# Start, bank choice, weight splits, filler transposes and a tail order changed together in a one-core decoder kernel

## The chip, the cores and the metric

The kernel runs on one core of a Trainium2 chip. The metric is the device time of one execution in microseconds (us); before the change its median over three runs is 1117.82 us (1117.63 to 1119.79).

The engines are named as in the profile: PE (TensorE matmul) with PEld (its weight loads), DVE (VectorE), ACT (ScalarE), POOL (GpSimd) and SP (SyncE, which here only issues DMAs).

## The reference

Two decoder layers on 256 tokens of width 1024. Each layer is FFN, mixer, FFN, per-layer input embedding, and each of the four is followed by a layer norm. The mixer of layer 0 is forgetting attention (16 heads of 64), that of layer 1 multi-head latent attention (16 heads of 128 + 64). All is float32.

```python
for i in range(DEPTH):                       # DEPTH = 2
    if i == N_A:                             # N_A = 1
        k_nope, k_rope, v_shared = shared_kv(x, ...)
    x = post_norm(x, 0.5 * swiglu(x, ffn1_w_in[i], ffn1_w_out[i]), ...)
    mix = fox_mixer(x, ...) if i < N_A else mla_mixer(x, ...)
    x = post_norm(x, mix, ...)
    x = post_norm(x, 0.5 * swiglu(x, ffn2_w_in[i], ffn2_w_out[i]), ...)
    gate = sigmoid(x @ ple_w_gate[i] + ple_b_gate[i])
    x = post_norm(x, gate * (p[i] @ ple_w_proj[i]), ...)

# fox_mixer: q, k, v = parts of x @ w_in; cum = cumsum(log_sigmoid(f_logit + b_f))
#   w = softmax(causal(q.k / 8 + cum_q - cum_k));  out = (w @ v) @ w_o
# post_norm(x, d) = layer_norm(ALPHA * x + d);  swiglu = (silu(gate) * up) @ w_out
```

## The kernel before

**Three matmuls for one.** Every float32 operand is split into a high part (rounded to the fp32r format) and a low part (the rest); a product is high x high + high x low + low x high (`mm3`). For weights the split is `Stream.split` (L140 on ACT writes the high part, L141 on DVE the low part, which reads the high part); for activations it is `parts` (L429 on ACT, L430 on DVE). A unit of weights is 128x1024 elements; two units make a group, which is what one DMA (or a few) loads into one of three raw buffers.

**The planner.** The order of instructions on every engine is the order in which the Python code emits them. `Stream` decides while emitting where the splits go: `use(key)` makes sure that a unit is split (and splits on the spot what isn't), `pump()` is called after every `mm3` and splits the next unit if a free slot is there and its own rough clocks (`pe_t`, `act_t`, `dve_t`, `arrives`) say that its data has arrived and that ACT and DVE are not behind. There are ten slots `hl0` to `hl9` for split units, and the buffers `ota`, `otb`, `qk`, `fs` are lent to it where they are not needed. DMAs go out on SP in the order of `load`.

**The start.** `setup` issues the loads: x of token tile 0 (two halves), group 0 of the first FFN's input weights in four pieces, x of tile 1. `run` transposes x of tile 0 (`XT(0)`), then `ffn(..., cold=True)` runs `H(0, 0)` (weight chunk 0, tile 0; four units of 6 matmuls of 512 columns), with `XT(1)` after its third unit, then `H(0, 1)` on the same units, then chunk 1. `spin` runs matmuls on a zero tile.

**FFN.** Chunks 0 and 1 go through `H`, chunks 2 to 10 through `HT` in three groups, 96 matmuls of 256 columns each; between the groups stand the output products `W` (matmuls of 512 columns). At the start of the second and third group (`c == group[0] > 2`), `EDGE` gives a number of transposes of the identity that are thrown away.

**Forgetting attention** (`fox`). `V(n, t)` makes the values (n: half of the heads, t: token tile) in PSUM ring "h" (two banks). `gates` makes the forget gates; their pointwise chain (`s1` to `s6`, on ACT, DVE and POOL) is put into a background list of which one piece is emitted at each `use` and at two places of each `ws`. `gen_k(j)`, `gen_q(j)` make keys and queries of a pair of heads: 24 matmuls of 256 columns (`ws`), in ring "h" too, and a split of the result (`parts`). Then a loop over eight head pairs j emits, in this order: `gen_k(j+1)`; `T(j-1)`, the transposes of the probabilities of the pair before (L897, L424) and their `parts` into PT; `QK(j)`; `softmax(j)`; `gen_q(j+1)`; `AV(j-1)`. `softmax` is: masked maxima on DVE (L865), bias (L872, L873), four exponentials on ACT (L877), one reciprocal of the four sums on DVE (L882), four multiplications on POOL (L886). In the last round and behind it the output products `O(k, t)` take the place of `gen`.

**Latent attention** (`mla`). A loop over 16 heads of the same kind (L1164, L1168, L1173, L1175 are its softmax); behind it comes a tail:

```python
self.load_gb(li, 1)
O(LATE + 2, (1,))
O(14, (0,))
T(15)
AV(15)
O(LATE + 3, (1,))
O(15, (0,))
```

The functions that the change touches:

Of the kernel before, what the change touches and what calls it, by code (L numbers as in the profile page):

```python
# [10 lines left out]
F32 = mybir.dt.float32  # L11
# [18 lines left out]
STAG = 3  # L30
LATE = 6
HAT = 12
VAT = 12
SW_COLD = 0
SW_H00 = 0
SW_H10 = 1
SW_H01 = 2
# [9 lines left out]
    (((0, 0),), ((1, 0),), ((0, 1),)),  # L47
)
GROUPS = ((2, 3, 4), (5, 6, 7), (8, 9, 10))
EDGE = {(0, "ffn1"): 4, (0, "ffn2"): 1, (1, "ffn1"): 2, (1, "ffn2"): 1}  # L50
VT = {0: (2, (0,)), 5: (2, (1,)), 8: (3, (0,)), 10: (3, (1,))}


# [13 lines left out]
class Recorder:  # L67
# [7 lines left out]
    def pump(self, *a, **k):  # L75
        pass

    lend = reclaim = check = load = busy = pair = pump


class Stream:


    def __init__(self, nc, raw_pool, pool, loads, seq):
        self.nc, self.raw_pool, self.pool, self.loads = nc, raw_pool, pool, loads
        seen = []
        self.groups = []
        for key in seq:
            g = group_of(key)
            if g not in seen:  # L90
# [20 lines left out]
        self.arrives = {}  # L111

    def load(self, n=NRAW):
        while self.loaded < len(self.groups) and self.loaded < self.done + n:
            g = self.groups[self.loaded]
            r = self.raw_pool.tile([128, 2048], F32, name="raw")
            self.loads(self.nc.sync, g, r, self.loaded < 2)
# [5 lines left out]
    def split(self):  # L123
# [16 lines left out]
        nc.scalar.activation(hi, src, AF.Copy)  # L140
        nc.vector.tensor_tensor(lo, src, hi.bitcast(F32), op=ALU.subtract)  # L141
        self.pair(n)
        self.hl[key] = w
# [43 lines left out]

    def pump(self):

        if self.ready == len(self.order) or not self.slots:  # L190
            return
        arrival = self.arrives.get(group_of(self.order[self.ready]), 1e12)
        if arrival <= self.pe_t + 500 and max(self.act_t, self.dve_t) <= self.pe_t + SLACK_NS:
            self.split()
# [29 lines left out]
def unit_of(key, raw):  # L224
# [5 lines left out]
        return raw[:, 1024 * u : 1024 * u + 1024], 128, 1024  # L230
    if k in ("fk", "fq"):
        return raw.rearrange("p (k c) -> p k c", c=256)[:, :, 128 * u : 128 * u + 128], 128, 1024
    if k == "ff":
        return raw[:, 0:1024], 128, 1024
    if k == "pb":
        return raw[0:1, 0:1024], 1, 1024
    if k == "kd":
        return raw[:, 640 * u : 640 * u + 640], 128, 640
    if k == "dq":
# [10 lines left out]
def make_loads(a):  # L250
    def rows(ap, k0, n):
        return ap[k0 * 128 : (k0 + n) * 128, :].rearrange("(k p) c -> p k c", p=128)

    def loads(q, g, raw, fine):
        k, i = g[0], g[-1]
        if k == "win":
            w = a[g[2]][0][g[1]]
            c = g[3]
            r = raw.rearrange("p (k c) -> p k c", c=512)
            n = 2 if fine else 4  # L260
            for k0 in range(0, 4, n):
                for s in range(2):
# [73 lines left out]
class Trunk:  # L336
# [33 lines left out]
    def setup(self):  # L370
# [6 lines left out]
        self.ones = one([1, 128], F32R, "ones")  # L377
        self.xT = one([128, 2, 2, 8, 128], F32R, "xT")
        self.rope = one([128, 2, 2, 64], F32, "rope")
        self.load_x(0)  # L380
        self.S.load(1)
        self.load_x(1)
        nc.gpsimd.memset(self.mask, 0.0)
        self.spin(2)
        warm = self.tl([128, 1], F32, "ss", 2)
        nc.gpsimd.memset(self.mhalf, -0.5)
# [17 lines left out]
    def load_x(self, t):  # L404
        for h in range(2):
            self.dma(
                self.x[t][:, 512 * h : 512 * h + 512],
                None if self.rec else self.a["x"][0, 128 * t : 128 * t + 128, 512 * h : 512 * h + 512],
            )


    def mm3(self, out, lhsT, rhs, start, stop):
# [17 lines left out]
        self.nc.vector.tensor_tensor(lo, src, hi.bitcast(F32), op=ALU.subtract)  # L430
        self.S.pair(cols(src))

    def transposed(self, t, src):

        for h in range(2):
# [10 lines left out]
    def XT(self, t):  # L446
        self.transposed(t, self.x[t])

    def moving(self, ps, t, name, width, at=None, what=None, sweeps=0):

# [58 lines left out]
    def ffn(self, li, which, lni, kv=False, at=None, cold=False):  # L509
# [7 lines left out]
        def H(c, t, at=None, what=None, sweeps=0):  # L517
            ps = self.bank("h")
            self.moving(ps, t, ("win", li, which, c), 512, at, what, sweeps)
            if c not in g:  # L520
                g[c] = self.tl([128, 768], F32, "P", 2)
            gt = g[c][:, 256 * t : 256 * t + 256]
# [57 lines left out]
        if kv:  # L580
            self.kv_down(0)
        if cold:
            H(0, 0, 18, lambda: self.XT(1), SW_COLD)
            H(0, 1, sweeps=SW_H01)
            H(1, 0)
        else:
            H(0, 0, sweeps=SW_H00)
# [131 lines left out]
    def fox(self, li):  # L719
# [11 lines left out]
        def ws(key, out):  # L731
            w = self.use(key)
            for k in range(8):
                if k in (3, 6) and self.bg:
                    self.bg.popleft()()
                self.mm3(
                    out, lambda i: w[:, i, 128 * k : 128 * k + 128],
                    lambda i: self.xT[:, :, i, k, :], k == 0, k == 7,
                )

        fs = self.own([128, 2048], F32, "fs")
        bf = self.tl([128, 1], F32, "bf", 1)
# [81 lines left out]
        def gen(j, key, c0):  # L824
            ps = self.bank("h")
            ws((key, j), ps[:, 0:256])
            o = qk[:, j % 2]
            self.parts(o[:, 0, c0 : c0 + 256], o[:, 1, c0 : c0 + 256], ps[:, 0:256])

        def gen_k(j):  # L830
            gen(j, "fk", 256)

        def gen_q(j):
            gen(j, "fq", 0)

        def QK(j, ring):
            sb = [self.bank(ring) for _ in range(2)]
# [17 lines left out]
        def softmax(j):  # L855
# [26 lines left out]
            nc.vector.reciprocal(su, su)  # L882
            for s in range(2):
                for q, (c0, c1) in enumerate(seg):
                    i = 2 * s + q
                    nc.gpsimd.tensor_scalar(  # L886
                        P[s][:, c0:c1], P[s][:, c0:c1], su[:, i : i + 1], 1.0, op0=ALU.mult, op1=ALU.mult
                    )
            st[j] = P

        def T(j):
# [52 lines left out]
        for j in range(8):  # L944
            if j == 2:
                self.load_gb(li, 1)
            if j < 7:
                gen_k(j + 1)
            else:
# [5 lines left out]
                S.lend("fs")  # L955
            if j >= 1:
                T(j - 1)
            QK(j, "y" if j < 7 else "h")
            softmax(j)
            if j < 7:  # L960
                gen_q(j + 1)
            else:
                O(2, 0)
                O(3, 0)
            if j >= 1:
                AV(j - 1)
        S.lend("qk")
        O(4, 0)
        O(5, 0)
# [80 lines left out]
    def mla(self, li):  # L1050
# [221 lines left out]

    def run(self):
        S = self.S
        self.XT(0)
        self.spin(2)
# [74 lines left out]
```

## Time and profile before

| | us |
|---|---|
| median of three runs | 1117.82 |
| the profiled execution, its own time | 1116.59 |
| its span, first to last instruction | 1114.8 |
| PE busy | 1087.3 |
| PEld busy | 982.3 |
| DVE busy | 712.2 |
| ACT busy | 541.6 |
| POOL busy | 81.8 |

The profiled execution took 1.8 us more than its span and 1.2 us less than the median. PE's matmuls overlap in the records, so PE busy time counts a stretch of back-to-back matmuls as full, at whatever rate they run; the number of matmuls in a stretch shows the rate. In a row of the timeline stand the start, the length, the engine, the line, the operation, output <- inputs, the shape and the count, and in brackets the idle time before it with what ended that.

Where the stages lie (us from the start of the span): first FFN 0 to 190, forgetting attention 190 to 320, second FFN 320 to 510, embedding 510 to 545, first FFN of layer 1 545 to 730, latent attention 730 to 890, second FFN 890 to 1075, embedding to the end.

### The profile page before, as it was taken

The page shows a single profiled execution, that of the slowest core. Times are in us where ns is not written, and L with a number is a line of the kernel's source. Part 1 is how long each engine was busy: PE and PEld are TensorE (multiplying, and loading weights), DVE is VectorE, ACT ScalarE, POOL GpSimd, SP SyncE. Part 2 cuts the span into 40 slices and gives each one's busy share as a digit, 9 for nine tenths or more (in the row PEclk, how much of TensorE's full clock was granted, in tenths as well). Part 3 has the DMA queues.
Part 4 walks back from the last instruction along what each step waited for, and adds up shares of the span by engine and source line. Part 5 has one row for each costly group of instructions (what it writes and reads, how often), then busy time and mean ns, then how long its engine had stood idle before and what let it go on. Part 6 is the DMA issues. An engine that isn't in the chain of part 4 may idle for free. (4 is left out here: it accounts for less than half of the span.)

```text
span 1114.8 us, 17666 instructions
## 1 busy us (share of the span) xinstructions
PE 1087.3 (98%) x7182; PEld 982.3 (88%) x7182; DVE 712.2 (64%) x994; ACT 541.6 (49%) x786; POOL 81.8 (7%) x130
## 2 busy tenths in 40 slices
PE   8999999989999999999999999998999899999997
PEld 6999998889879989897899899987899689898986
DVE  5765545777787555457976454397766786454576
ACT  5554433566646435443565343345655455344421
POOL 0000000322200000000320000011111000000000
PEclk9999999989999999999999999999999999999999
DMA  9796652554338666454486655344443478555402
GB/s 299 240 308 212 216 188 68 171 168 152 114 113 301 200 209 199 159 175 157 155 287 229 204 186 166 88 111 145 156 123 114 158 257 278 185 190 189 164 26 76
DMA packets 150548, 199.00 MB, mean 179 GB/s; under 512 B 11714, under 2 KB 128450, under 8 KB 150468
## 3 DMA queue, kind: packets, MB, share of 16 engines
q1 hardware_dynamic: 150468, 197.88, 53.8%
q8 instruction: 56, 0.92, 0.3%
q14 instruction: 24, 0.20, 0.1%
HBM read 196.81 MB, written 1.05 MB: 177 GB/s over the span
## 5 line engine op out<-in xcount | busy, mean ns | idle before, releaser
L141 DVE TENSOR_TENSOR hl<-raw,hl 128x1024 fp32r<-128x1024 f32 (+3 forms) x295 | 349.3, 1202 | 184.8 <-ACT hl L140 183.7
L140 ACT ACTIVATE hl<-raw 128x1024 fp32r<-128x1024 f32 (+3 forms) x295 | 298.5, 1032 | 208.0 <-PE y L420 85.3
L420 PE MATMUL h<-xT,hl 128*128 128x256 f32 x2016 | 243.3, 281 | 2.4 <-DVE g L430 1.8
L420 PEld LDWEIGHTS h<-xT,hl 128*128 128x128 f32 x2016 | 237.4, 190 | 4.7 <-DVE g L430 2.0
L420 PE MATMUL y<-hl,g 128*128 128x512 f32 x816 | 189.6, 390 | 0.0
L420 PEld LDWEIGHTS y<-hl,g 128*128 128x128 f32 x816 | 152.2, 188 | 31.0
L420 PE MATMUL h<-hl,xT 128*128 128x512 f32 (+1 forms) x432 | 102.1, 387 | 3.3 <-DVE hl L141 1.9
L420 PE MATMUL tr<-xT,hl 128*128 128x256 f32 x864 | 102.5, 278 | 0.0
L420 PEld LDWEIGHTS tr<-xT,hl 128*128 128x128 f32 x864 | 100.5, 188 | 0.1
L420 PEld LDWEIGHTS h<-hl,xT 128*128 128x128 f32 x432 | 79.3, 188 | 21.2 <-DVE hl L141 3.0
L492 POOL TENSOR_TENSOR rs<-ve,mhalf 128x1 f32<-128x1 f32 x16 | 15.2, 950 | 829.4 <-DVE ve L491 829.4
L420 PE MATMUL y<-hl,xT 128*128 128x512 f32 (+2 forms) x276 | 52.6, 346 | 0.0
L420 PEld LDWEIGHTS y<-hl,xT 128*128 128x128 f32 x276 | 44.0, 188 | 6.4 <-issue 0.7
L429 ACT ACTIVATE xT<-tr 128x512 fp32r<-128x512 f32 x36 | 20.0, 596 | 57.0 <-PE tr L424 57.0
L430 DVE TENSOR_TENSOR g<-P,g 128x512 fp32r<-128x512 f32 x36 | 24.9, 693 | 34.5 <-ACT g L429 34.5
L429 ACT ACTIVATE g<-P 128x512 fp32r<-128x512 f32 x36 | 22.8, 632 | 40.1 <-DVE P L559 29.1
L420 PE MATMUL y<-hl,ota 128*128 128x512 f32 x144 | 36.1, 394 | 0.0
L141 DVE TENSOR_TENSOR otb<-raw,otb 128x1024 fp32r<-128x1024 f32 (+1 forms) x20 | 24.1, 1203 | 18.8 <-ACT otb L140 18.8
L141 DVE TENSOR_TENSOR qk<-raw,qk 128x1024 fp32r<-128x1024 f32 x21 | 25.9, 1233 | 14.3 <-ACT qk L140 14.3
L420 PE MATMUL tr<-xT,qk 128*128 128x256 f32 x264 | 31.9, 277 | 0.0
L420 PEld LDWEIGHTS tr<-xT,qk 128*128 128x128 f32 x264 | 30.9, 188 | 0.0
L430 DVE TENSOR_TENSOR xT<-tr,xT 128x512 fp32r<-128x512 f32 x36 | 23.1, 683 | 11.7 <-ACT xT L429 11.7
(222 smaller groups left out, 1349.2 us busy)
## 6 DMA issues: line engine op xcount, KB each, us to landing
raw<-in_ffn_w_in_dram SPq DMA_DIRECT2D x172, 512.0 KB, 4.9
raw<-in_ffn_w_out_dram SPq DMA_DIRECT2D x44, 1024.0 KB, 5.1
raw<-in_fox_w_in_dram SPq DMA_DIRECT2D x12, 1024.0 KB, 5.2
raw<-in_ple_w_gate_dram SPq DMA_DIRECT2D x8, 1024.0 KB, 5.0
raw<-in_mla_w_o_dram SPq DMA_DIRECT2D x8, 1024.0 KB, 5.5
gb<-in_ln_g_dram SPq DMA_DIRECT2D x8, 512.0 KB, 5.1
gb<-in_ln_b_dram SPq DMA_DIRECT2D x8, 512.0 KB, 7.7
raw<-in_fox_w_o_dram SPq DMA_DIRECT2D x4, 1024.0 KB, 4.8
```

Of the source, the lines that this page charges most:

```text
L140: nc.scalar.activation(hi, src, AF.Copy)
L141: nc.vector.tensor_tensor(lo, src, hi.bitcast(F32), op=ALU.subtract)
L420: self.nc.tensor.matmul(out, lhsT, rhs, start=start, stop=stop)
L429: self.nc.scalar.activation(hi, src, AF.Copy)
L430: self.nc.vector.tensor_tensor(lo, src, hi.bitcast(F32), op=ALU.subtract)
L492: nc.gpsimd.tensor_tensor(rs, ve, self.mhalf, op=ALU.pow)
```

## The change

Seven edits in one:

1. **Loads at the start.** The first two groups are loaded in pieces of one 128-row block (128 KB) instead of two; both groups are issued at once, with the four halves of x between their pieces (x tile 0 half 0 first, then blocks 0 and 1, x tile 1 half 0, blocks 2 and 3, x tile 0 half 1, block 4, x tile 1 half 1, blocks 5 to 7).
2. **`first()`** takes the place of `H(0, 0)` and `H(0, 1)`: it goes through the eight blocks with both token tiles by turns, transposes x by halves, and splits the first four units in two pieces each (`FINE`), with planned splits held.
3. **`V` for t = 1** uses a bank of ring "y" (four banks) instead of "h".
4. **Splits in the forgetting attention set by hand.** `QUIET` and `hold` keep `pump` from splitting in `gates`, `gen_k(0)`, `gen_q(0)`, the later part of `gen_k(1)`, `gen_q(1)`, and in the whole loop from j = 1. Instead, in each round one unit is split whole just ahead of the first matmuls of `gen_k` (`split_now`, from `gen_k(2)` on), and another in two halves: the high part on ACT behind `T(j-1)` (`ahead`), the low part on DVE behind the reciprocals and multiplications of `softmax(j)` (`later`). In the last round one split stands between `O(2, 0)` and `O(3, 0)`.
5. **The reciprocal** is done in two pieces, one for each head of the pair, each followed by that head's multiplications.
6. **`EDGE` of layer 1's first FFN** is 4 instead of 2.
7. **The tail of the latent attention** runs `T(15)`, `O(LATE + 3, (1,))`, `AV(15)`, `O(14, (0,))`, `O(15, (0,))`.

```diff
+FINE = 4
+QUIET = {("ff", 0): 0, ("fk", 0): 0, ("fq", 0): 0, ("fk", 1): 3, ("fq", 1): 0}
-EDGE = {(0, "ffn1"): 4, (0, "ffn2"): 1, (1, "ffn1"): 2, (1, "ffn2"): 1}
+EDGE = {(0, "ffn1"): 4, (0, "ffn2"): 1, (1, "ffn1"): 4, (1, "ffn2"): 1}
...
+    def ahead(self):
+        if self.ready == len(self.order) or not self.slots or self.rest is not None:
+            return
+        if self.arrives.get(group_of(self.order[self.ready]), 1e12) <= self.pe_t + 500:
+            self.split(half=True)
+    def split_now(self):
+        self.ahead()
+        self.later()
+    def later(self):
+        if self.rest is not None:
+            f, self.rest = self.rest, None
+            f()
...
+        if self.ready < FINE:
+            part(slice(0, 1))
+            between()
+            part(slice(1, 2))
+        elif half:
+            nc.scalar.activation(hi, src, AF.Copy)
...
+            self.rest = rest      # the low part on DVE, emitted by later()
+            return
+        else:
+            part(slice(None))
...
     def pump(self):
-        if self.ready == len(self.order) or not self.slots:
+        if self.ready == len(self.order) or not self.slots or self.hold:
...
-        self.load_x(0)
-        self.S.load(1)
-        self.load_x(1)
+        self.load_x(0, 0)
+        self.S.between = {(0, 2): lambda: self.load_x(1, 0),
+            (1, 0): lambda: self.load_x(0, 1), (1, 1): lambda: self.load_x(1, 1)}
+        self.S.load(2)
...
+        def first():
+            S.hold = True
+            self.XT(0, (0,))
+            self.spin(2)
+            S.split()
+            part(0, 0, 1)
+            S.split(lambda: self.XT(1, (0,)))
+            part(0, 2)
+            part(1, 0, 1)
+            S.split(lambda: self.XT(0, (1,)))
+            part(1, 2)
+            part(0, 3)
+            part(1, 3)
+            self.XT(1, (1,))
+            S.split()
+            part(0, 4, 5, 6, 7)
+            act(0, 0, ps[0])
+            part(1, 4, 5)
+            S.split()
+            S.split()
+            S.hold = False
+            part(1, 6, 7)
+            act(0, 1, ps[1])
...
-            ps = self.bank("h")                       # V
+            ps = self.bank("h" if t == 0 else "y")
...
+                S.hold = hold or k >= QUIET.get(key[:1] + key[-1:], 8)      # ws
...
-            nc.vector.reciprocal(su, su)
+            def divide(s):
+                nc.vector.reciprocal(su[:, 2 * s : 2 * s + 2], su[:, 2 * s : 2 * s + 2])
...
+            divide(0)
+            divide(1)
+            S.later()
...
+            S.hold = j >= 1                            # the loop over head pairs
...
                 T(j - 1)
+                if j < 7:
+                    S.ahead()
...
                 O(2, 0)
+                S.split_now()
                 O(3, 0)
...
         O(LATE + 2, (1,))                              # tail of mla
+        T(15)
+        O(LATE + 3, (1,))
+        AV(15)
         O(14, (0,))
-        T(15)
-        AV(15)
-        O(LATE + 3, (1,))
         O(15, (0,))
```

More of the change, by code (lines that the diff above doesn't have):

```diff
@@ L76, in pump @@
         pass
-    lend = reclaim = check = load = busy = pair = pump
+    lend = reclaim = check = load = busy = pair = split = ahead = later = split_now = pump
+    between, hold = {}, False
 class Stream:
@@ L111, in __init__ @@
         self.arrives = {}
+        self.between = {}
+        self.hold = False
+        self.rest = None
     def load(self, n=NRAW):
@@ L116, in load @@
             r = self.raw_pool.tile([128, 2048], F32, name="raw")
-            self.loads(self.nc.sync, g, r, self.loaded < 2)
+            self.loads(self.nc.sync, g, r, self.loaded < 2, self.between)
             self.raw[g] = r
@@ L121, in load, with split @@
             self.loaded += 1
-    def split(self):
+    def ahead(self):
[10 more added lines that the diff above has]
+            f()
+    def split(self, between=lambda: None, half=False):
+        self.later()
         nc = self.nc
@@ L252, in rows, with loads @@
         return ap[k0 * 128 : (k0 + n) * 128, :].rearrange("(k p) c -> p k c", p=128)
-    def loads(q, g, raw, fine):
+    def loads(q, g, raw, fine, between):
         k, i = g[0], g[-1]
@@ L259, in loads @@
             r = raw.rearrange("p (k c) -> p k c", c=512)
-            n = 2 if fine else 4
+            n = 1 if fine else 4
             for k0 in range(0, 4, n):
+                if fine and (i, k0) in between:
+                    between[i, k0]()
                 for s in range(2):
@@ L431, in parts, with transposed @@
         self.S.pair(cols(src))
-    def transposed(self, t, src):
-        for h in range(2):
+    def transposed(self, t, src, halves=(0, 1)):
+        for h in halves:
             tr = self.bank("tr")
@@ L519, in H, with part, act @@
             self.moving(ps, t, ("win", li, which, c), 512, at, what, sweeps)
+            act(c, t, ps)
+        def first():
+            ps = [self.bank("h") for _ in range(2)]
+            def part(t, *ks):
+                for k in ks:
+                    w = self.use(("win", li, which, 0, k // 2))
+                    for i, j in SWEEPS[0][0]:
+                        self.mm(
+                            ps[t], self.xT[:, t, i, k, :], w[:, j, 512 * (k % 2) : 512 * (k % 2) + 512],
+                            k == 0 and (i, j) == (0, 0), k == 7 and (i, j) == SWEEPS[0][0][-1],
+                        )
+                    self.S.pump()
+            S.hold = True
[20 more added lines that the diff above has]
+            act(0, 1, ps[1])
+        def act(c, t, ps):
             if c not in g:
@@ L582, in ffn @@
         if cold:
-            H(0, 0, 18, lambda: self.XT(1), SW_COLD)
-            H(0, 1, sweeps=SW_H01)
+            first()
             H(1, 0)
@@ L729, in V, with ws @@
             v[t, n] = o
-        def ws(key, out):
+        def ws(key, out, at={}, hold=False):
             w = self.use(key)
             for k in range(8):
+                if k in at:
+                    at[k]()
+                S.hold = hold or k >= QUIET.get(key[:1] + key[-1:], 8)
                 if k in (3, 6) and self.bg:
@@ L739, in ws @@
                 )
+            S.hold = hold
         fs = self.own([128, 2048], F32, "fs")
@@ L966, in fox @@
                 AV(j - 1)
+        S.hold = False
         S.lend("qk")
```

48 lines of the change are left out of this document (28 added, 20 removed).

## The prediction

> **What bounds the kernel now.** I read the page first, then the table of busy time by stretches of 20 us, then the timeline of PE wherever a stretch was not full or its matmuls were few for its length, and last the rows of DVE, ACT and POOL around each hole.
>
> ```profile
> span 1114.8 us, 17666 instructions
> PE 1087.3 (98%) x7182; PEld 982.3 (88%) x7182; DVE 712.2 (64%) x994; ACT 541.6 (49%) x786; POOL 81.8 (7%) x130
> ...
> 0.00:20.00 20.00, 15.54 (x60) 10.51 (x61) 9.68 (x11) 11.06 (x15) 1.75 (x11) 1.00 0.94 307
> 220.00:240.00 20.00, 17.68 (x140) 16.83 (x138) 14.84 (x30) 11.28 (x23) 3.78 (x6) 0.91 0.65 211
> ```
>
> PE is 98% busy, and nothing in the change removes a product: only holes, slow stretches and fillers on PE can be won. In each row the first number behind the length is PE's busy time. Of 20.00 us PE worked 15.54 at the start and 17.68 at 220, where forgetting attention begins. The number behind the five engines is the granted clock: 0.91 at 220.
>
> **1. The start.**
>
> ```profile
> 0.72 0.87 SPq L358 DMA_DIRECT2D x<-in_x_dram  x2
> x<-in_x_dram SPq DMA_DIRECT2D x1, 256.0 KB, 2.6
> 4.77 1.09 ACT L429 ACTIVATE xT<-tr 128x512 fp32r<-128x512 f32 x2 [2.56 <-PE tr L424]
> 6.52 1.06 ACT L140 ACTIVATE hl<-raw 128x1024 fp32r<-128x1024 f32 x1 [0.67 <-DMA raw<-in_ffn_w_in_dram]
> 7.63 0.50 PE L420 MATMUL h<-hl,xT 128*128 128x512 f32 x1 [1.17 <-ACT hl L140]
> 15.10 1.03 PE L424 MATMUL tr<-ident,x 128*128 128x128 f32 x8
> 15.89 18.10 PE L420 MATMUL h<-hl,xT 128*128 128x512 f32 x78
> ```
>
> Each unit's split waits for its DMA, and PE for the split. From 15.89 on PE runs through at 18.10/78 = 0.232 us a matmul; 30 of these (6 of `H(0, 0)`, 24 of `H(0, 1)`) end the first two products at 22.9.
>
> After: the first half of x lands where it does now, 0.72 + 2.6 = 3.3; its ACT eviction starts at 4.77 and is half as long, to 5.3. Block 0 needs 512 KB landed; 256 KB were there at 3.3 and 1 MB at 6.5, so about 4.4 by interpolation. Half a unit on ACT is about 0.55: first matmul at 5.9 instead of 7.63. From there lie 48 matmuls (11.1) and 12 transposes (1.03/8 each, 1.5) on PE, 18.5 in all. Followed through step by step, PE still waits some 0.9 us, mostly at block 6, whose split stands behind the fourth x eviction on ACT. So 19.4 to 19.5 against 22.9: **gain 3.3**. The twenty smaller DMAs cost about 0.45 of SP's time each (0.87/2), 9.7 us for all, and with 2.6 of landing the last arrives near 13, where it does now. If these small pieces land 2 us late, 1.2 stays; PE never waiting would give 4.3.
>
> **2. `V` in ring "y", and `QUIET`.**
>
> ```profile
> 220.15 2.91 PE L420 MATMUL h<-xT,hl 128*128 128x256 f32 x24
> 224.84 7.35 PE L420 MATMUL h<-xT,hl 128*128 128x256 f32 x48 [1.78 <-DVE g L430]
> 233.40 5.73 PE L420 MATMUL h<-xT,hl 128*128 128x256 f32 x48
> 224.11 0.68 DVE L430 TENSOR_TENSOR g<-h,g 128x512 fp32r<-128x512 f32 x1
> 227.16 0.42 DVE L430 TENSOR_TENSOR qk<-h,qk 128x256 fp32r<-128x256 f32 x1
> 224.00:230.00 6.00, 5.16 (x31) 5.16 (x32) 5.84 (x10) 3.80 (x6) 0.00 (x0) 0.72 0.63 192
> ```
>
> `gen_q(0)` wants the bank of `V(1, 1)`, whose low part DVE does only at 224.11, behind gate arithmetic and two splits: PE stands 1.78. Then the granted clock over 6 us is 0.72, and the next 48 matmuls take 7.35 where the same 48 later take 5.73: 1.62 more. With `V` in "y" that wait has no cause. Next late is `gen_k(1)`, due at about 220.15 + 2 x 2.73 = 225.6, which wants the bank of `gen_k(0)`: its low part, 0.42, comes behind the row at 224.11, two gate rows and a copy, near 226.3 without the split that stands between the gate rows now. So 0.7 stays: **gain 1.8 + 1.6 - 0.7 = 2.7** (1.1 if the clock drops all the same, 3.4 if nothing is late). Behind `gen_k(1)` are only the queue of PE and, on DVE, work for `QK(0)`, due later.
>
> **3. The first round of the softmax.**
>
> ```profile
> 238.25 3.65 POOL L886 TENSOR_SCALAR P<-P,su 128x128 f32<-128x128 f32 x4 [15.14 <-DVE su L882]
> 304.44 1.62 POOL L886 TENSOR_SCALAR P<-P,su 128x128 f32<-128x128 f32 x4 [6.47 <-DVE su L882]
> 238.97 0.50 PE L897 MATMUL tr<-ident,P 128*128 128x128 f32 x2
> 241.50 0.78 PE L897 MATMUL tr<-ident,P 128*128 128x128 f32 x2 [2.03 <-POOL P L886]
> 243.62 4.47 PE L420 MATMUL h<-xT,hl 128*128 128x256 f32 x24
> 262.08 3.01 PE L420 MATMUL h<-xT,hl 128*128 128x256 f32 x24
> 242.00:248.00 6.00, 6.00 (x42) 5.61 (x43) 4.58 (x17) 3.09 (x11) 0.08 (x1) 0.72 0.50 175
> 238.85 1.30 DVE L141 TENSOR_TENSOR hl<-raw,hl 128x1024 fp32r<-128x1024 f32 x1 [0.77 <-ACT hl L140]
> ```
>
> PE's `T(0)` waits 2.03 and some 0.3 more for POOL's third and fourth multiplications, and again a stretch at the lower clock follows (4.47 for 24 matmuls against 3.01: 1.46). The four take 3.65 where 1.62 is enough (the row at 304.44). With the reciprocal in two, the first head's two multiplications start 0.8 earlier, all four are through at about 239.1, about when the low part that begins at 238.85 could hold them, against 241.9. `T(0)` is due at 238.97; some 0.3 may stay where DVE is later with the maxima. **Gain 2.3 + 1.5 - 0.3 = 3.5** (low 1.0: a wait of 1.3 and the clock stay; high 3.8).
>
> **4. The rounds from j = 4 on.**
>
> ```profile
> L886 POOL TENSOR_SCALAR P<-P,su 128x128 f32<-128x128 f32 x1 | 1.3, 1336 | 0.0
> 266.94 0.18 DVE L882 RECIPROCAL su<-su 128x4 f32<-128x4 f32 x1 [1.11 <-ACT P L877]
> 267.82 1.29 DVE L141 TENSOR_TENSOR hl<-raw,hl 128x1024 fp32r<-128x1024 f32 x1 [0.70 <-ACT hl L140]
> 264.76 0.37 ACT L877 ACTIVATE P<-y,tt 128x128 f32<-128x128 f32 x1 [2.93 <-DVE tt L873]
> 260.26 0.60 PE L897 MATMUL tr<-ident,P 128*128 128x128 f32 x4
> 268.81 0.38 PE L897 MATMUL tr<-ident,P 128*128 128x128 f32 x2
> 278.12 0.38 PE L897 MATMUL tr<-ident,P 128*128 128x128 f32 x2
> 296.79 0.38 PE L897 MATMUL tr<-ident,P 128*128 128x128 f32 x2
> ```
>
> From one `T` to the next a round takes 8.55 where PE doesn't wait (260.26 to 268.81) and 9.31 where it does (268.81 to 278.12; to 296.79 two more of 9.33). DVE sets that: it works through but for 1.11 waiting for the exponentials and 0.70 waiting for the high part of the split. The high part goes to where ACT is idle (2.93 before the first exponential), so the 0.70 goes and a round on DVE is 9.33 - 0.70 = 8.65 with the second reciprocal (0.18) mostly in the 1.11. The four rounds that wait lose 0.8 each now, 0.1 to 0.2 then: **gain 2.6** (0.8 to 3.2).
>
> What speaks against it: while DVE's low part runs, POOL's third multiplication takes 1.336 instead of about 0.37, and now the low part comes straight behind the reciprocal, ahead of it. I take that the whole 1.2 is lost to POOL there; the second head is then ready at about 269.1 against 269.8 now, just behind `T`, which is the 0.1 to 0.2. The Trainium skill, "SBUF — State Buffer", section "Who interferes with whom", says the same: a DVE instruction with two SBUF inputs and a GpSimd one that reads SBUF exclude each other for a whole instruction, by order of issue. The trace agrees (1.336 beside a low part); without that rule nothing would stay and the sum would be 0.6 better.
>
> **5. `EDGE` 2 to 4.**
>
> ```profile
> 94.75 0.60 PE L424 MATMUL tr<-ident 128*128 128x128 f32 x4
> 106.09 11.04 PE L420 MATMUL h<-xT,hl 128*128 128x256 f32 x96
> 632.49 0.38 PE L424 MATMUL tr<-ident 128*128 128x128 f32 x2
> 705.83 11.47 PE L420 MATMUL h<-xT,hl 128*128 128x256 f32 x96
> ```
>
> The same 96 matmuls take 11.04 behind four fillers (layer 0) and 11.47 behind two (layer 1). Six chunks of layer 1 run at the slower rate: 6 x 0.43 = 2.6, less four more fillers of 0.11 (0.60 - 0.38 for two): **gain 2.15** if the rate is set by the fillers, -0.44 if not. I take the gain, since both groups of layer 0 with the same four run fast. Other groups may change their rate as well, 1.3 a group either way; I take none.
>
> **6. The tail.**
>
> ```profile
> 871.08 1.59 PE L420 MATMUL y<-hl,ota 128*128 128x512 f32 x6
> 872.66 0.82 POOL L1175 TENSOR_SCALAR P<-P,su 128x128 f32<-128x128 f32 x2 [6.69 <-DVE su L1173]
> 879.79 1.53 PE L420 MATMUL y<-hl,fs 128*128 128x512 f32 x6
> ```
>
> `O(14)` waits for the evictions of `AV(14)`, and `AV(15)` for those of `T(15)` with nothing between. After: `T(15)` waits for POOL to 873.5, `O(LATE + 3)` covers its evictions to 875.2, their low part is there at 875.5 to 876.6 (a planned split ahead of it or not), so the last product starts at 877.7 to 878.8 instead of 879.79. **Gain 1.3** (1.0 to 2.1; -0.5 if two planned splits stand ahead of PT on ACT and DVE).
>
> **The sum.** 3.3 + 2.7 + 3.5 + 2.6 + 2.15 + 1.3 = 15.6. The profiled execution took 1116.59, so 1101.0; the median of the runs is 1.2 above it: **1102 us**. The lows together give 1.2 + 1.1 + 1.0 + 0.8 - 0.4 - 0.5 = 3.2, the highs 4.3 + 3.4 + 3.8 + 3.2 + 2.15 + 2.1 = 19.
>
> **The rivals.** *The clock.* The stretches at the lower clock may not come from the waits. They would stay: 1.6 + 1.5 less, 1105. For: after four waits of 0.8 in the rounds there is none, so a wait alone doesn't do it. Against: both stand right behind the two longest waits. The Trainium skill, "TensorE: Matmul & The Clock Gate", Part 1, says that about 3.4 us of idle are needed; here 1.78 and 2.03 went ahead of a drop, so the trace doesn't bear that out.
>
> *POOL and DVE keep the rounds bound.* If low parts hold POOL's multiplications as long as at 238.25 (3.65 for 1.62), parts 3 and 4 give their lows: 1106.3. Against: only one split stands behind the reciprocals.
>
> *The waits only move*: to DMA landing at the start, from `T` to `QK`, or `EDGE` changes no rate; the lows: 1114 to 1115.
>
> *Slower: the loop runs out of split weights.* With planned splits off, `use` must split on the spot what isn't ready, PE standing for 1.06 + 1.23 = 2.3. Two units are needed and two split in a round, so this decides only if `ahead` finds no slot or no data in most rounds; then from j = 4 eight units cost 18.4, and part 4 is lost: 1102 + 18.4 + 2.6 = 1123. Against: the ten slots hold the units up to at least `fq(3)` before the loop holds the planner off, and a unit's group is loaded two groups, so about two rounds, before it is split.
>
> **How the numbers follow.** Forecast 0.62 (1098.5 to 1106), clock 0.12, POOL and DVE 0.12, waits moved 0.07, slower 0.04, better than 1098 0.03. The likeliest is 1102; 1097 to 1110 leaves out most of the moved waits, the slower and the best, 0.15 in all. A measurement here tells 0.2%, 2.2 us: faster 0.90, same 0.05, slower 0.05.
>
> **What would show it.** First matmul of weights near 6 us and chunk 1 from 19.5; no wait on `g` at 222; clock 1.00 there; `T` to `T` of 8.6 to 8.7 in all rounds; chunks of 11.04 in layer 1; 8 us or less from `O(LATE + 2)` to the last product of the tail's half. It is wrong if DVE rows of L141 inside the rounds stand ahead of the maxima, or if PE waits for L141 in `gen_k`.

## The result and the profile after

| | before | after |
|---|---|---|
| median of four runs, us (lowest to highest) | 1118.59 (1117.63 to 1119.79) | 1100.39 (1099.47 to 1102.1) |
| ratio after/before, 95% interval | | 0.984 [0.982, 0.985] |
| the profiled execution, its own time / span | 1116.59 / 1114.8 | 1102.1 / 1100.3 |
| PE / DVE / ACT / POOL busy | 1087.3 / 712.2 / 541.6 / 81.8 | 1080.1 / 711.5 / 542.5 / 79.7 |

The change made the kernel 18.2 us faster, 1.6%; predicted were 1102 and a range of 1097 to 1110. The two profiled executions differ by 14.5 us of span. The forecast of 1101.0 for the profiled execution met 1102.1.

The page after the change, and the same two stretches of busy time (behind the length: PE, PEld, DVE, ACT and POOL busy with their counts, the granted clock, the share of DMA, GB/s):

```profile
span 1100.3 us, 17702 instructions
PE 1080.1 (98%) x7186; PEld 976.7 (89%) x7186; DVE 711.5 (65%) x1006; ACT 542.5 (49%) x790; POOL 79.7 (7%) x130
...
0.00:20.00 20.00, 18.43 (x70) 12.45 (x71) 8.88 (x14) 10.39 (x17) 1.76 (x11) 1.00 0.87 275
220.00:240.00 20.00, 19.38 (x173) 18.47 (x172) 14.97 (x44) 11.92 (x30) 3.39 (x7) 1.00 0.46 148
```

PE works 18.43 of the first 20 us (15.54 before) and 19.38 of the twenty from 220 (17.68 before), there at full clock (0.91 before).

The timeline of forgetting attention after, PE first, then one round on DVE and POOL:

```profile
224.31 3.01 PE L469 MATMUL h<-xT,hl 128*128 128x256 f32 x24 [0.62 <-DVE qk L479]
234.10 0.60 PE L994 MATMUL tr<-ident,P 128*128 128x128 f32 x4
242.65 0.60 PE L994 MATMUL tr<-ident,P 128*128 128x128 f32 x4
...
257.03 0.17 DVE L976 RECIPROCAL su<-su 128x2 f32<-128x2 f32 x1 [0.93 <-ACT P L969]
257.11 1.20 DVE L175 TENSOR_TENSOR hl<-raw,hl 128x1024 fp32r<-128x1024 f32 x1
265.48 0.17 DVE L976 RECIPROCAL su<-su 128x2 f32<-128x2 f32 x1 [0.93 <-ACT P L969]
265.57 1.21 DVE L175 TENSOR_TENSOR hl<-raw,hl 128x1024 fp32r<-128x1024 f32 x1
264.65 0.83 POOL L979 TENSOR_SCALAR P<-P,su 128x128 f32<-128x128 f32 x2 [5.63 <-DVE su L976]
265.74 1.73 POOL L979 TENSOR_SCALAR P<-P,su 128x128 f32<-128x128 f32 x2 [0.26 <-DVE su L976]
```

No `T` waits. The one wait on DVE in a round is 0.93 for the exponentials, and its round is 265.48 - 257.03 = 8.45, just under PE's 8.54. POOL's second pair takes 1.73 beside the low part where the first takes 0.83, and is done at 267.47; `T` wants it at 268.26. The times from one `T` to the next, worked out from the unrounded starts of the `T` rows (L897 before, L994 after, L995 in r10):

| round from `T(j)` to `T(j+1)` | 0 | 1 | 2 | 3 | 4 | 5 | 6 | sum |
|---|---|---|---|---|---|---|---|---|
| before | 12.75 | 8.54 | 8.55 | 9.31 | 9.39 | 9.28 | 9.47 | 67.29 |
| after | 8.55 | 8.54 | 8.54 | 8.54 | 8.54 | 8.43 | 8.50 | 59.64 |
| r1, planner | 8.55 | 11.34 | 9.73 | 9.33 | 9.32 | 9.96 | 9.31 | 67.54 |
| r2, one reciprocal | 11.81 | 8.54 | 8.54 | 8.56 | 8.73 | 9.01 | 8.64 | 63.82 |
| r3, low part at once | 8.54 | 8.54 | 8.69 | 9.16 | 9.15 | 10.21 | 8.51 | 62.80 |
| r10, both parts late | 8.54 | 8.54 | 8.54 | 8.79 | 9.30 | 10.01 | 9.30 | 63.02 |

### The profile page after: what moved, and what is told of

The parts are those of the page before. It is cut to its first block, busy times and chain, and to the rows that moved or that the text cites. A ratio compares the mean times of both kernels' runs of the same rounds, so it can differ in the third digit from the quotient of the medians.

```text
span 1100.3 us, 17702 instructions
## 1 busy us (share of the span) xinstructions
PE 1080.1 (98%) x7186; PEld 976.7 (89%) x7186; DVE 711.5 (65%) x1006; ACT 542.5 (49%) x790; POOL 79.7 (7%) x130
## 3 DMA queue, kind: packets, MB, share of 16 engines
HBM read 196.81 MB, written 1.05 MB: 180 GB/s over the span
## 5 line engine op out<-in xcount | busy, mean ns | idle before, releaser
L164 DVE TENSOR_TENSOR hl<-raw,hl 128x1024 fp32r<-128x1024 f32 (+3 forms) x287 | 334.5, 1184 | 172.5 <-ACT hl L163 171.7
L163 ACT ACTIVATE hl<-raw 128x1024 fp32r<-128x1024 f32 (+3 forms) x287 | 286.9, 1021 | 198.6 <-PE y L469 82.2
L469 PE MATMUL h<-xT,hl 128*128 128x256 f32 x2016 | 239.9, 278 | 1.7 <-DVE P L613 0.7
L469 PEld LDWEIGHTS h<-xT,hl 128*128 128x128 f32 x2016 | 234.1, 188 | 3.7 <-DVE P L613 0.9
L469 PE MATMUL h<-hl,xT 128*128 128x512 f32 (+1 forms) x396 | 94.7, 388 | 0.4 <-DVE hl L164 0.3
L469 PEld LDWEIGHTS h<-hl,xT 128*128 128x128 f32 x396 | 72.1, 188 | 17.1 <-DVE hl L164 2.2
L469 PE MATMUL y<-hl,xT 128*128 128x512 f32 (+2 forms) x312 | 61.0, 351 | 0.0
L469 PEld LDWEIGHTS y<-hl,xT 128*128 128x128 f32 x312 | 50.8, 188 | 7.9 <-issue 0.7
```

What stands on the lines that cost most here:

```text
L163: nc.scalar.activation(hi[:, c], src[:, c], AF.Copy)
L164: nc.vector.tensor_tensor(lo[:, c], src[:, c], hi[:, c].bitcast(F32), op=ALU.subtract)
L469: self.nc.tensor.matmul(out, lhsT, rhs, start=start, stop=stop)
```

## The experiments

Each undoes or shifts one part of the changed kernel. A median moves by up to 2 us for reasons that lie elsewhere (end of this part), so each is read first from its own stage in the trace, against the changed kernel.

| run | what | in its stage, us | median, us | ratio to before, 95% |
|---|---|---|---|---|
| r1 | planner in the loop | +7.9 | 1106.87 | 0.992 [0.989, 0.994] |
| r2 | one reciprocal | +4.2 | 1103.56 | 0.988 [0.986, 0.991] |
| r3 | low part at once | +3.2 | 1101.85 | 0.987 [0.985, 0.989] |
| r4 | `V` in "h" | +2.8 | 1100.80 | 0.986 [0.984, 0.988] |
| r5 | old start | +1.7 | 1101.14 | 0.987 [0.985, 0.988] |
| r6 | two fillers | +2.2 | 1102.17 | 0.987 [0.986, 0.989] |
| r7 | old tail | +3.7 | 1102.83 | 0.988 [0.987, 0.990] |
| r8 | four fillers, third groups | -2.5 | 1100.00 | 0.986 [0.984, 0.987] |
| r9 | wait filled | +4.2 | 1102.63 | 0.987 [0.985, 0.989] |
| r10 | both parts late | +3.4 | 1102.86 | 0.988 [0.986, 0.990] |
| r11 | three additions | see there | 1100.88 | 0.986 [0.983, 0.988] |
| r12 | changed kernel again | | 1098.74 | 0.984 [0.982, 0.986] |

**r1, the planner back in the loop.**

```diff
-            gen(j, "fk", 256, {0: S.split_now} if j >= 2 else {}, j >= 2)
+            gen(j, "fk", 256)                     # and gen_q alike
...
-            S.hold = j >= 1
...
-                if j < 7: S.ahead()
...
-                S.split_now()
```

> The loop of the forgetting attention gives its splits back to the planner (no hold, no split set by hand); the reciprocal in two, QUIET, V in ring y and all else stay as changed. Theory A (a round is bound by DVE, and the 0.70 us that DVE stood for the high part of a split was what made it so): from the third or fourth round on T to T is 9.1 to 9.3 us again instead of 8.54, with T waiting for POOL or DVE; the kernel is 2.0 to 3.5 us slower than the changed one. Rival B (the reciprocal in two frees POOL early enough by itself, the place of the splits is nothing): T to T 8.54 to 8.6 in all rounds, no wait at T, within 0.5 us.

DVE in the second round, from `T(1)` to `T(2)`:

```profile
242.47 0.17 DVE L976 RECIPROCAL su<-su 128x2 f32<-128x2 f32 x1 [0.96 <-ACT P L969]
243.42 1.23 DVE L164 TENSOR_TENSOR fs<-raw,fs 128x1024 fp32r<-128x1024 f32 x1 [0.78 <-ACT fs L163]
244.56 1.22 DVE L164 TENSOR_TENSOR hl<-raw,hl 128x1024 fp32r<-128x1024 f32 x1
246.91 2.36 DVE L164 TENSOR_TENSOR hl<-raw,hl 128x1024 fp32r<-128x1024 f32 x2
```

Theory A's mark is there: 0.78 of DVE waiting for the high part and rounds of 9.3. But the loss is 7.9, not 2.0 to 3.5. In the second round the planner puts four splits on DVE (4.8 us), ahead of the evictions that PE waits for: 11.34. The kernel before had one split there and 8.54. r1 differs from it by `QUIET` and the other edits too, and why its planner puts four there is not shown. Rival B falls: with the reciprocal in two and the planner in the loop, the seven rounds take 67.54, no better than before (67.29).

**r2, one reciprocal.**

```diff
-                nc.vector.reciprocal(su[:, 2 * s : 2 * s + 2], su[:, 2 * s : 2 * s + 2])   # in divide(s)
...
+            nc.vector.reciprocal(su, su)                                                   # ahead of divide(0)
```

> The reciprocals of both heads in one instruction again, the splits set by hand stay. With one reciprocal POOL's first multiplication begins some 0.8 us later, at the time when the low part (1.2 us) begins on DVE, so that POOL's multiplications run beside it and not ahead of it. Theory A (the splits carry the rounds, the reciprocal only the first softmax round): T to T at most 0.2 us longer, 0 to 1.2 us in all rounds, and T(0) waits 0.3 to 1.0 us. Rival B (the two edits need each other, since the low part directly behind one reciprocal holds all four multiplications): P is ready 0.5 to 1.0 us behind T in every round, T to T 9.0 to 9.5, 3 to 6 us slower than the changed kernel.

PE at `T(0)`, and DVE and POOL in a later round:

```profile
235.73 0.33 PE L994 MATMUL tr<-ident,P 128*128 128x128 f32 x1 [1.09 <-POOL P L978]
237.27 4.62 PE L469 MATMUL h<-xT,hl 128*128 128x256 f32 x24
260.24 1.20 DVE L175 TENSOR_TENSOR hl<-raw,hl 128x1024 fp32r<-128x1024 f32 x1
260.42 2.51 POOL L978 TENSOR_SCALAR P<-P,su 128x128 f32<-128x128 f32 x4 [6.20 <-DVE su L982]
```

Theory A's order of sizes: the later rounds are 0 to 0.6 longer (A allowed 0.2 each), 0.9 in sum, and `T(0)` waits 1.09. What A missed is the stretch at half clock behind that wait (4.62 for 24 matmuls that take 3.01 otherwise); wait and half clock make the first round 3.3 longer. So the 4.2 lies in the range of rival B, but not by B's way: most rounds are not late. From r1 and r2 together: taken from the finished kernel, the reciprocal in two costs 4.2 and the splits by hand 7.9, in sum 12.1, where the rounds of before and after differ by 7.65. So the two do not add up. How the 7.65 divide between them is not shown: in r1 the first round keeps what the reciprocal gains (8.55 against 12.75 before) and the rounds behind it lose as much again, and the reciprocal in two as the only edit of the old kernel was not run.

**r3 and r10, the two halves of the split moved one at a time.**

```diff
-                    S.ahead()                 # r3: low part right behind the high part, behind T
+                    S.split_now()
...
-                    S.ahead()                 # r10: high part right ahead of the low part
-            S.later()                         # end of softmax
+            if 1 <= j < 7: S.split_now()
```

> Only the low part is moved: it is emitted on DVE directly behind its high part (behind T, ahead of the maxima) instead of behind the reciprocals. It then waits for the high part, and the maxima begin some 1.2 to 1.5 us later, but POOL is no longer held beside it (the second head's two multiplications 0.83 instead of 1.73). Theory A (DVE's order decides by where it leaves a wait, and the low part in front costs what POOL gains): T to T 8.54 to 8.85, 0 to 2 us slower than the changed kernel. Rival B (the maxima are the start of the chain to T, so all that is put ahead of them is paid): T to T 9.2 or more, 4 us or more slower.

> The other half of the hand-set split is moved: its high part is not ahead of the maxima on ACT but behind the exponentials, directly ahead of its low part behind the reciprocals. Theory A (the step of the prediction: DVE stands 0.7 to 0.9 us for the high part there, and has only 8.54 - 7.32 - 0.93 = 0.29 us to spare in a round): T to T 9.0 to 9.3 from the round on in which the slack is used up, 2 to 3.5 us slower than the changed kernel, though POOL is not held (0.83 for two). Rival B (it was POOL's being held that bound the rounds): POOL done 0.9 earlier, T to T stays 8.54.

DVE and POOL in a round, r3 and then r10:

```profile
260.58 0.86 DVE L1023 TENSOR_TENSOR ota<-y,ota 64x256 fp32r<-64x256 f32 x2 [0.22 <-ACT ota L1020]
261.66 1.23 DVE L175 TENSOR_TENSOR hl<-raw,hl 128x1024 fp32r<-128x1024 f32 x1 [0.23 <-ACT hl L171]
269.07 0.83 POOL L979 TENSOR_SCALAR P<-P,su 128x128 f32<-128x128 f32 x2 [0.26 <-DVE su L976]
```

```profile
259.89 1.23 DVE L175 TENSOR_TENSOR hl<-raw,hl 128x1024 fp32r<-128x1024 f32 x1 [0.78 <-ACT hl L171]
268.52 0.82 POOL L979 TENSOR_SCALAR P<-P,su 128x128 f32<-128x128 f32 x2 [0.27 <-DVE su L976]
```

In both POOL runs free (0.83 for its second pair instead of 1.73), and both are slower. In r10 DVE stands 0.78 for the high part and its round goes from 8.45 to 9.3, as A said. In r3 the high part is no longer waited for behind the reciprocals; instead DVE comes too early to `AV`'s evictions and to the next split and stands 0.22 + 0.23 for ACT there, which is most of the 0.70 by which its round is longer (9.15 against 8.45). Rounds of 9.15 are near rival B's 9.2, above A's 8.85; the loss of 3.2 lies between the two. So the low part behind the reciprocals does two things: its own high part has long been written, and its 1.2 us are the time that ACT needs for the evictions that DVE wants next. That POOL is held for 0.9 us by it costs nothing, since POOL has 0.8 left to `T`.

**r4, `V` for tile 1 in "h" again.** The edit is `self.bank("h")` in `V`.

> V for token tile 1 in ring h again; QUIET and all else as changed. gen_q(0) wants the bank of V(1, 1) again, whose low part DVE does behind gate arithmetic. Theory A (a wait for this bank, then a stretch at half clock behind it): a wait of 1 to 2 us ahead of gen_q(0) and the next 48 matmuls 7.3 instead of 5.7 us, the wait of 0.62 at gen_k(1) gone: 2.0 to 2.8 us slower than the changed kernel. Rival B (the stretch at half clock does not come from the wait): the wait alone, less the 0.62: 0.4 to 1.3 us slower. Rival C (QUIET alone brought the low part forward): no wait over 0.3 us, no change.

```profile
223.00 7.35 PE L469 MATMUL h<-xT,hl 128*128 128x256 f32 x48 [1.78 <-DVE g L479]
```

Theory A: the row of before is back number for number, wait and half clock, and `T(0)` is 2.8 us later, the later start of this profile (0.26) taken off. `QUIET` alone does nothing for it.

**r5, the old start.** Loads, `XT`, `H(0, 0)`, `H(0, 1)` and `FINE = 0` as before.

> The start as before the change: loads in pieces of two blocks, x of tile 1 behind group 0, XT(0) first, H(0, 0) and H(0, 1) in place of first(), no split in two pieces; all else as changed. Theory A (the start gains by itself what the two traces differ by at the first evicted transposes, 2.1 us, and all of it is kept): the transposes at 31.74 come at 33.8 again, and every later stage 2.0 to 2.2 us later. Rival B (the start only moves a wait: the planner, held in the changed start, catches up later): the difference is down to 0 to 1 us by 190 us.

```profile
8.03 0.50 PE L467 MATMUL h<-hl,xT 128*128 128x512 f32 x1 [1.08 <-ACT hl L163]
```

Weights from 8.03 instead of 6.22; the first evicted transposes come 1.74 later (33.48), and all through the next 160 us it stays at 1.68 to 1.69. A is right that nothing is given back, 0.3 to 0.5 below the size it gave. This start itself varies: those transposes stand at 31.45 to 32.43 in the profiles of the new start, so that against single ones of these profiles r5 is 1.05 to 2.03 later.

**r6, two fillers** (`(1, "ffn1"): 2`) **and r8, four for every third group** (`4 if c == 8 else EDGE[li, which]`).

> EDGE of layer 1's first FFN is 2 again, all else as changed. Theory A (the fillers set the rate of the 96 matmuls of a chunk for the whole group): six chunks of 11.47 us instead of 11.04 in layer 1's first FFN, 6 x 0.43 less four fillers of 0.11, 2.1 us longer there. Rival B (the rate comes from the state in which PE arrives, and the fillers are only one of its causes): one group or none goes slow, 0 to 1.1 us.

> The third group of HT chunks takes four fillers in every FFN; the second groups and all else as changed. It is aimed at the third group of both second FFNs, which runs its 288 matmuls at 117.8 ns in the changed kernel and at 113.3 in the one before. Theory A (the fillers set the rate): both groups at 113.3, 288 x 4.5 ns = 1.3 us each, less three more fillers of 0.11 each: 0.9 to 1.0 us shorter in each second FFN, 1.8 to 2.0 in all. Rival B (the rate is set by how the wait for the eviction at the second unit falls, not by the fillers): the groups stay at 117.8 and each stage is 0.33 us longer, 0.7 in all.

A chunk of layer 1's first FFN in the changed kernel and in r6; then the third group of layer 0's second FFN in the changed kernel, in r8, and in r12, the changed kernel run again:

```profile
691.77 11.04 PE L469 MATMUL h<-xT,hl 128*128 128x256 f32 x96
```

```profile
692.80 11.47 PE L469 MATMUL h<-xT,hl 128*128 128x256 f32 x96
```

```profile
451.60 8.04 PE L469 MATMUL h<-xT,hl 128*128 128x256 f32 x66 [0.20 <-ACT ota L736]
```

```profile
450.96 8.58 PE L469 MATMUL h<-xT,hl 128*128 128x256 f32 x72
```

```profile
451.45 7.76 PE L469 MATMUL h<-xT,hl 128*128 128x256 f32 x66 [0.19 <-ACT ota L736]
```

r6 answers with all six chunks at 11.47 and 2.14 us: theory A. r8 has both third groups at the quicker rate, 1.24 us shorter each. That is more than expected: the fillers stand in the place of the 0.2 for `ota` and cost nothing (33.25 from the first filler to the end of the group, as in r12 with one). But r12, the same program as the changed kernel, has them quick as well. With one filler ahead of it, the rate of this group is a matter of the execution: both were slow in three of twelve profiles (the changed kernel's first, r1, r2) and quick in the rest. So what r8 cures is a chance; two profiles with four fillers (r8, r11), both quick, don't settle how surely.

**r7, the old tail.**

> The tail of the latent attention in the old order, O(14), T(15), AV(15), O(LATE + 3), O(15), all else as changed. Theory A (O(LATE + 3) between T(15) and AV(15) hides the evictions): from O(LATE + 2) to the last product of this half 1.2 us longer. Rival B (the waits of the changed kernel, 0.42 at T(15) and 1.04 at AV(15), come from planned splits and not from the order, and the old order finds others): within 0.4 us.

The changed kernel's PE in the tail, and two stretches of r7:

```profile
858.32 0.90 PE L473 MATMUL tr<-ident,P 128*128 128x128 f32 x3 [0.42 <-POOL P L1277]
861.78 0.79 PE L469 MATMUL h<-PT,g 128*128 128x256 f32 x5 [1.04 <-DVE PT L479]
```

```profile
855.00:861.00 6.00, 4.46 (x18) 2.87 (x17) 4.36 (x7) 3.88 (x8) 0.83 (x2) 0.87 0.33 94
861.00:867.00 6.00, 5.35 (x18) 4.07 (x16) 1.16 (x3) 1.37 (x3) 0.00 (x0) 0.56 1.03 354
```

From `O(LATE + 2)` to the end of `O(15)` it is 12.59 in r7, 8.89 in the changed kernel and 10.07 before. r7 is 3.7 longer, of which about 2.5 are a stretch at half clock that the kernel before did not have on the same waits; the 1.2 of the order remain.

**r9, the wait of r4 filled with matmuls.** `V` is in "h" again as in r4, and besides:

```diff
         gen_k(0)
+        self.spin(8)
         gen_q(0)
```

> As r4_v_in_h (V for token tile 1 in ring h, so that gen_q(0) stands for about 1.8 us), with eight matmuls of 384 columns on the zero tile put ahead of gen_q(0), 8 x 0.171 = 1.4 us of PE work that nobody reads. The wait for the bank stays, PE's idle time in it goes from 1.78 to about 0.4 us. Theory A (the clock is granted in steps of 3.413 us, and a step is halved when PE idled in about half of the step before, 1.7 us or more): no step at half clock at 224, the 48 matmuls behind it 5.7 us instead of 7.35; T(0) 1.0 to 1.2 us later than in the changed kernel instead of 2.8. Rival B (the drop comes with what ends or causes the wait, not with idle time): the 48 matmuls take 7.35 again, T(0) 2.8 us later.

```profile
220.48 5.32 PE L452 MATMUL y<-mask 128*128 128x384 f32 x16
225.35 5.92 PE L469 MATMUL h<-xT,hl 128*128 128x256 f32 x48
```

The eight count as sixteen in the trace, 0.33 us each: 5.32 us, not 1.4. They cover the wait whole and 3 us more, so `T(0)` is 4.2 later, the earlier start of this profile (0.29) taken off. No half clock follows, but as no wait is left either, A and B are not told apart here.

**r11, three additions, beside r12, the changed kernel.** `gen_k(0)` in ring "tr", four fillers for every third group, and the planner held from `O(LATE, (1,))` to `AV(15)`.

> The changed kernel with three additions: four fillers ahead of the third group of HT in every FFN; gen_k(0) in a bank of ring tr, so that gen_k(1) does not wait for DVE's low part (0.62); the planner held in the tail of the latent attention from O(LATE, (1,)) to AV(15), so that no planned split stands ahead of T(15)'s POOL work and of PT's low part (0.42 + 1.04). Theory A (these waits are held up by nothing else): 0.6 + 1.2 to 1.5 us, and up to 2.5 where the third groups would have run slow: 2 to 4 us faster than the changed kernel, about 1097.5. Rival B (the splits that are held are missed behind the tail: the next FFN's first chunk waits for its weights): as fast as the changed kernel or up to 2 us slower.

> The changed kernel itself beside r11_three_more, for the comparison: 1099.5 to 1102. If the rate of the third groups is a matter of the execution and not of the program, some of its runs are about 2.5 us apart, and this profile may show them at 113.3 ns a matmul where the first showed 117.8.

PE in r11 behind the tail:

```profile
858.68 0.80 PE L469 MATMUL h<-PT,g 128*128 128x256 f32 x6
870.91 0.63 PE L473 MATMUL tr<-ident,x 128*128 128x128 f32 x4 [0.89 <-DVE x L546]
881.19 1.21 PE L469 MATMUL h<-hl,xT 128*128 128x512 f32 x4 [0.92 <-ACT hl L163]
884.95 3.04 PE L469 MATMUL h<-hl,xT 128*128 128x512 f32 x12 [1.68 <-ACT hl L163]
```

The wait of 0.62 is gone (0.9 won at `T(0)`, the later start of this profile taken off) and `AV(15)`'s 1.04 too, but rival B decides: the splits held in the tail are missed in the next FFN, 0.92 + 1.68 for weights. The 0.89 for x is new as well; how much of it comes from the held splits was not worked out. r11 takes 1100.88 where the changed kernel beside it takes 1098.74. The same without the hold was not run. So no version here has a lower median than the changed kernel.

**What moves a median.** The slow third groups are 2.5 us a run, a stretch at half clock is 1.7, the start varies by 1. This is the likely reason why the medians of r4, r5 and r8 don't stand where their stages alone would put them.

## Why the prediction was right, and where its steps were not

| step | predicted | before against after | undone |
|---|---|---|---|
| 1 start | 3.3 | 2.1 | 1.7 (r5) |
| 2 `V`, `QUIET` | 2.7 | 2.8 | 2.8 (r4) |
| 3 first softmax round | 3.5 | 4.2 | 3.3 (r2) |
| 4 later rounds | 2.6 | 3.45 | with 3: 7.9 (r1) |
| 5 `EDGE` | 2.15 | 2.14 | 2.14 (r6) |
| 6 tail | 1.3 | 1.2 | 1.2 without the half clock (r7) |
| sum | 15.6 | 15.9 | |

*The start* is the term that was most mis-sized. These rows of the changed kernel show it, of PE, ACT and the list of DMAs:

```profile
3.91 1.06 PE L473 MATMUL tr<-ident,x 128*128 128x128 f32 x4
5.01 0.60 ACT L478 ACTIVATE xT<-tr 128x512 fp32r<-128x512 f32 x1 [2.79 <-PE tr L473]
7.72 0.63 ACT L163 ACTIVATE hl<-raw 128x512 fp32r<-128x512 f32 x1 [0.71 <-DMA raw<-in_ffn_w_in_dram]
10.65 0.63 ACT L163 ACTIVATE hl<-raw 128x512 fp32r<-128x512 f32 x1 [0.53 <-DMA raw<-in_ffn_w_in_dram]
6.22 2.30 PE L469 MATMUL h<-hl,xT 128*128 128x512 f32 x6
16.54 5.78 PE L469 MATMUL h<-hl,xT 128*128 128x512 f32 x24 [0.30 <-DVE hl L164]
raw<-in_ffn_w_in_dram SPq DMA_DIRECT2D x16, 128.0 KB, 3.7
```

The first matmul is at 6.22, not 5.9, as the first eviction is a quarter microsecond later and halves of units take 0.60 to 0.63 on ACT, not 0.55. The quarter does not come from the change. The four transposes of x ahead of the eviction run at half rate in this execution (1.06, against 0.60 for four of them at 8.36). The trace's record of the granted clock begins with the full clock, here at 5.50, before at 4.36. In r5, the old start, it begins at 5.34 and the eviction is at 5.01 as well; in r6, the new start, it begins at 4.28, and the eviction is at 4.74. These are r6's rows:

```profile
3.91 0.79 PE L473 MATMUL tr<-ident,x 128*128 128x128 f32 x4
5.90 2.43 PE L469 MATMUL h<-hl,xT 128*128 128x512 f32 x6
```

So 5.9 holds for an execution with an early full clock, like the one that it was worked out from. Behind the first matmul PE loses 1.8, not 0.9: 31 of the 48 matmuls lie ahead of 16.54, the other 17 end at 16.54 + 17 x 5.78/24 = 20.6, and 6.22 + 12.6 would be 18.8. The pieces of 128 KB take 3.7 from issue to landing where 2.6 was assumed, and ACT waits 0.71 and 0.53 for them: the stated doubt about small pieces landing late, at about half its size.

*Step 3*: a stretch at half clock lasts 3.41 us and costs 1.7; the prediction read 1.46 from one group of 24. With the wait of 2.3 that makes 4.0 of the measured 4.2, and the 0.3 that was to stay did not. *Step 4*: DVE's round was put at 8.65 with the low part holding POOL until 269.1. It is 8.45, since the wait for the exponentials shrank from 1.11 to 0.93 as well and the split beside the reciprocals from 1.29 to 1.21; POOL is done 0.8 ahead of `T`. Nothing stays of the 0.1 to 0.2. The Trainium skill's rule that was cited there ("SBUF — State Buffer", "Who interferes with whom") holds: POOL's second pair takes 1.73 against 0.83. But r3 and r10, in which POOL is free and the rounds are longer, show that this was not what bound them.

*Rivals*: the one of the clock falls with r4 and r2, where the waits come back and the half clock with them. The one of split weights running out falls too: the only listed wait of the changed kernel's PE for a low part of weights is the 0.30 at 16.54. One sign of being wrong was badly chosen: in each round a low part stands ahead of the maxima, that of the split ahead of `gen_k` (at 259.45), and one stood there before (260.85). The sum came out right by luck in part: the errors of steps 1, 3 and 4 (-1.2, +0.7, +0.85) nearly cancel. The rest of the span went as it came, and was taken as none: +1.15 where the first group of layer 0's second FFN turned quick, and -1.24 twice where the third groups turned slow: 15.9 - 1.3 = 14.6 of the 14.5.

## What to carry to other kernels

When an in-order engine has just enough time for a round, place a long piece of free work where its own input has been ready for long and where the work behind it needs time on another engine: here behind the reciprocals, worth 0.6 to 0.8 us a round against either neighbouring place. Don't sum such edits: the two that share a round cost 4.2 and 7.9 when undone one at a time, and were worth 7.65 together. To divide a gain between them, add each to the old kernel as well as undoing it from the finished one; here the first half of that is missing. And holding work off a stretch moves it to the next, which in r11 had less room than the stretch it was taken from.

## What the runs showed of the hardware that was not expected

**The clock is halved in steps of 3.413 us on a fixed raster.** Every stretch at half clock inside the kernels lasted 3.413 us or twice that, and within a profile they start whole multiples of 3.413 apart (226.23, 243.29 and 775.77 before: 5 and 156 steps between them). Two steps each of before, r9 and r12, cut at these borders (for r12, which has no half clock inside, they are counted back from the stretch at half clock that ends its profile):

```profile
222.82:226.23 3.41, 1.62 (x15) 1.43 (x14) 3.31 (x6) 3.06 (x6) 0.29 (x1) 1.00 0.67 205
226.23:229.64 3.41, 3.41 (x19) 3.41 (x18) 3.35 (x5) 1.21 (x3) 0.00 (x0) 0.50 0.73 258
```

```profile
760.33:763.74 3.41, 2.12 (x17) 1.65 (x16) 2.92 (x4) 3.07 (x6) 0.65 (x2) 1.00 0.12 35
763.74:767.15 3.41, 3.41 (x19) 3.41 (x18) 2.25 (x8) 1.11 (x5) 0.00 (x0) 0.50 0.84 185
```

```profile
757.14:760.55 3.41, 2.18 (x16) 1.83 (x16) 3.41 (x6) 2.22 (x5) 0.00 (x0) 1.00 0.33 90
760.55:763.97 3.42, 2.63 (x21) 2.34 (x20) 1.94 (x7) 1.97 (x6) 0.65 (x2) 1.00 0.84 223
```

The same wait in latent attention (1.24 for a low part) halved the next step in before, r4 and r9 and in none of the other eleven profiles: it is the idle time that falls within one step that counts. Added up from all matmuls, as the time between two starts beyond a matmul's length at full rate, PE had idled 1.78 us or more in the step ahead of each halved one, and at most 1.73 in the other steps at full clock but one (1.82): about half of a step. That is observed over fourteen profiles, not shown by an experiment. It would explain why waits of 1.09 (r2) can cost 1.7 us more and 1.04 (the tail after) nothing. The Trainium skill, "TensorE: Matmul & The Clock Gate", Part 1, has the window (3413 ns, free-running); its need of a whole idle window is not what these runs show.

**256-column matmuls run at 113.3 or 117.8 ns, and a whole group keeps the rate with which it begins**, 11.04 or 11.47 for 96. In every group that had four transposes ahead of it the rate was the quicker one; in layer 1's first FFN, which had two of them before and in r6, it was the slower one in both groups. The number alone does not set it: with one filler both rates occur, and the first groups, which have none, are quick in all but two cases (layer 0's second FFN before, the last FFN in r10). What sets it stays open.
